# Ten of sixteen gates computed in pairs by seven block products, and a new order of the kernel's opening

## The chip, the cores and the metric

The kernel runs on one core of one Trainium2 chip. The metric is the device time of one execution in microseconds; the time before is the median of three runs, 1073.86 us (1072.72 to 1075.79). The engines are called by short names: PE (TensorE, the matrix products), PEld (its weight loads), DVE (VectorE), ACT (ScalarE), POOL (GpSimd) and SP (SyncE, whose queue issues every DMA of this kernel).

## The reference, cut to what matters

One layer of a hybrid decoder for 512 prompt tokens and 8 samples of 8 tokens, together 576 tokens, all in float32:

```python
h = rmsnorm(x, norm1_g)                       # 1024 channels
z = h @ w_in                                  # mLSTM, RWKV and gate columns
hm = mlstm(z[..., :M_END])  ;  y_a = hm @ w_branch_m
yr = rwkv7(z[..., R_START:R_END]) ; y_b = yr @ w_branch_r
gates = sigmoid(z[..., G_START:])             # 2 x 1024 columns
merged = gates[..., :1024] * y_a + gates[..., 1024:] * y_b
x = x + merged @ w_out
u = rmsnorm(x, norm2_g) @ f_up                # causal conv, gelu, gating
x = x + (gelu(conv(u[..., :D_FF])) * u[..., D_FF:]) @ f_down
x = x + sigmoid(rmsnorm(x, ple_norm_g) @ ple_gate_w) * (pe @ ple_proj)
```

followed by a last norm; the states of both branches are returned as well. The change touches the first norm, the first tiles of `h @ w_in`, and `gates`.

## The kernel before

**Layout.** Activations lie with channels on the 128 partitions and the 576 tokens along the free axis, in two halves of 288 columns (`HF`). The 1024 input channels are 8 blocks k. Each float32 operand is split into a high part and a low remainder (ACT casts the high part, DVE subtracts it), and a product takes three matrix products: high x high, high x low, low x high. `dense` computes one tile of 128 output channels: 8 blocks x 3 products x 2 halves, 48 products of 288 columns, into two PSUM banks. `wload` brings its weights in two pieces of 128x512 (256 KB each), casts (line 169) and subtracts (line 170).

**PSUM.** `bank(tag)` hands out banks by tag: three of `d`, two of `r`, and one each of `s`, `c` and `m`. In later stages the list `turn` rotates tag `d` over other tags; during the mixers it is empty.

**The opening** (lines 373 to 463). x comes in 16 loads of 144 KB (8 blocks, 2 halves). Three tiles of `w_in` lead: 12 and 13 (RWKV's low-rank columns) and 0. They are multiplied with x times the norm's gain, not yet normalised, and scaled by the norm's reciprocal root `rs` when they are evicted. Eight products on zeros (line 394) stand ahead. For each half, the squares of x are summed (ACT squares, POOL adds), `rms_half` adds them over the partitions by three one-column products, takes the root on POOL and spreads it by three transposes into a PSUM bank. Then `norm_half` writes the normalised and split x, `xs1`, and the two gate inputs of the mLSTM (`lps["if"]`, line 458) and tile 4 are computed from it.

**The mixers.** `PLAN` lists the steps in program order: `x a d b s c` with a pair's number are the RWKV steps of a pair of heads (inputs, preparation, the serial inverse of the diagonal blocks on DVE, the middle products, the samples, the output), `m` is an mLSTM head (four dense tiles and its chain), and `g` one gate tile. Sixteen gates i = 2m + b are dense tiles of `w_in`, whose result goes through tanh (line 1209) and a store (line 1210) to a buffer in device memory, `d_th[i]`, read back when the branches are merged. A gate depends on `xs1` alone, so it can stand wherever PE would otherwise wait. The order of the code sets priorities; a planner reorders the instructions of each engine when the kernel is built, by its own estimate of times. At run time each engine keeps that order.

**The buffers.** The RWKV steps use pool `rwkv` (`rp`), most tags with one buffer. `AR` and `bon` have two. `BK` is also used as `XA`, read by the middle products (line 809); `UVM` by the samples (line 886); `t1` to `t5`, `xr`, `xk`, `xv`, `xw`, `xa` by the preparation. After the plan the pool is closed and the branch stage's tiles lie in its memory.

**The FFN** already multiplies by seven block products (`seven`, from line 287). Two output tiles and two halves of the tokens form a 2x2 block matrix product with the two halves of the input channels; it takes 8 block products in the plain way and 7 by forming sums of weights (`plus`) and sums of inputs (`mixed`, line 274, once per stage). Each block product is 4 blocks x 3 products. The seven weights are split anew (lines 294 and 295), and the results are put together from banks by additions on DVE (lines 322, 327 and the caller's).

Of the kernel before, what the change touches and what calls it, by code (L numbers as in the profile page):

```python
# [15 lines left out]
P = 128  # L16
# [14 lines left out]
PLAN = "x0 a0 d0 x1 b0 a1 d1 s0 c0 g0 m0 b1 g1 x2 a2 d2 s1 c1 m1 g2 b2 x3 a3 d3 g3 s2 c2 b3 g4 g5 s3 m2 g6 c3 g7 m3 g8 g9 g10 g11 g12 g13 g14 g15".split()  # L31
# [64 lines left out]
def build(tc, nc, I, O):  # L96
# [12 lines left out]
    with st0:  # L109
# [119 lines left out]
        def rms_half(pl, acc, hf, pt="m"):  # L229

            pm = bank(pt)
# [7 lines left out]
            b = bank(pt)  # L239
# [34 lines left out]
        def mixed(tiles, pl, b11, b12, b21, b22, k, T4):  # L274

            n1, n2, t3, n4 = (pl.tile([P, HF], F32, tag=t, name="tt", bufs=2) for t in ("u2", "u2", "u3", "u3"))
# [4 lines left out]
            for name, t, e in (("n2", n2, V), ("n1", n1, G), ("t3", t3, V), ("n4", n4, V)):  # L281
                h, l = (tiles[name + a][:, k, :] for a in "hl")
# [4 lines left out]
        def seven(srca, srcb, x4, sp):  # L287
# [10 lines left out]
            def plus(a, b, e):  # L298
                t = sp.tile([P, 4, P], F32, tag="ws", name="ws", bufs=3)
                e.tensor_tensor(t, a, b, ALU.add)  # L300
                return t
# [7 lines left out]
            def tile(tag):  # L309
                return sp.tile([P, HF], F32, tag=tag, name=tag, bufs=2)  # L310

            a11, a21, a22, a12 = wdma8(srca, 0), wdma8(srcb, 0), wdma8(srcb, 4), wdma8(srca, 4)
            A, F, E, Dm = (bank("d", "pd") for _ in range(4))
            w11 = parts(a11)
            prod(A, w11, x4["b11"])
            u3 = tile("u3")
# [4 lines left out]
            u2 = tile("u2")  # L321
# [54 lines left out]
        with ExitStack() as stn:  # L376
# [14 lines left out]
            S.copy(warm[:, 0:1], nhalf)  # L391
# [17 lines left out]
            wdma(2, 0)  # L409
            wdma(2, 1)  # L410
# [3 lines left out]
            lws = [wsplit(raw[0], KD, npool, ("nh", "nl"), 6)]  # L414
            def raw_split(k, hf):
# [1104 lines left out]
```

## Time and profile before

| | |
|---|---|
| median of three runs | 1073.86 us |
| the profiled execution | 1070.66 us |
| its span, first to last instruction | 1068.8 us |
| mean granted clock of PE | 0.996 |
| PE busy | 1045.1 us, 98% |
| DVE busy | 777.0 us, 73% |
| ACT busy | 508.8 us, 48% |
| POOL busy | 254.5 us, 24% |
| DMA | 114.74 MB, mean 107 GB/s |

The profile is one execution, about 2 us longer than its span. Busy time of PE counts a product from issue to its modelled end, and products overlap, so two stretches that are both "busy" can hold different numbers of products. A group of instructions is shown by line, engine, operation and tile, with its count, its busy time, the mean of one, and what ended the idle time ahead of it. A window row gives, for one stretch, the busy time and count of each engine, the granted clock (1.00 is full), the share of the 16 DMA engines and the GB/s.

### The profile page before, as it was taken

What the parts mean: (1) busy time and instruction counts of PE and PEld (TensorE: products, weight loads), DVE (VectorE), ACT (ScalarE), POOL (GpSimd) and SP (SyncE); (2) the same over time, 40 slices, a digit from 0 to 9 for tenths busy, and PEclk for the clock granted to TensorE, in tenths of its full rate; (3) what the DMA queues carried; (4) which work ended last, traced back from release to release, by engine and by line L of the source; (5) the groups of instructions that cost most, each with busy time, mean ns of one, the idle gap of its engine ahead of it and who ended that gap; (6) DMA issues with size and microseconds to landing.
All of it is one profiled execution on the core that took longest, in us unless ns stands there. A gap on an engine that the chain in (4) does not pass through costs nothing.

```text
span 1068.8 us, 23108 instructions
## 1 busy us (share of the span) xinstructions
PE 1045.1 (98%) x8991; PEld 1009.0 (94%) x8991; DVE 777.0 (73%) x1645; ACT 508.8 (48%) x1072; POOL 254.5 (24%) x394
## 2 busy tenths in 40 slices
PE   8899999999999999999999999999999999999996
PEld 7899999999989988999999999999999999999996
DVE  7887657876786676356775799945998569975864
ACT  7684634462553344334343465522565236553822
POOL 7622112221131021001401253200343005410300
PEclk9999999999999999999999999999999999999999
DMA  7243412442342322446850312322233322342513
GB/s 252 95 127 93 108 53 58 103 141 60 88 143 75 81 84 91 143 151 234 263 181 1 116 37 93 110 90 75 85 99 97 102 70 90 94 117 67 165 40 123
DMA packets 90894, 114.74 MB, mean 107 GB/s; under 512 B 35617, under 2 KB 45217, under 8 KB 90785
## 3 DMA queue, kind: packets, MB, share of 16 engines
q1 hardware_dynamic: 90784, 113.27, 34.7%
q8 instruction: 70, 1.15, 0.4%
q14 instruction: 40, 0.32, 0.1%
HBM read 94.79 MB, written 18.45 MB: 106 GB/s over the span
## 4 chain that ended last, share of the span: by engine, by line
PE 90%; DVE 4%; DMA 4%; ACT 1%; issue 1%; SPq 0%; POOLq 0%; DVEq 0%; ACTq 0%
PE pd L193 55%; PE pd L306 20%; PE pm L655 1%; PE pm L1106 1%; PE pm L1136 1%; PE pm L835 1%; PE pm L809 1%; DMA yin<-d_y 1%; PE pm L910 1%; DVE xnf L268 1%; PE pm L917 1%; PE pm L1199 1%; PE pm L775 0%; DMA d_y<-og 0%; DMA wr<-i_w_out 0%
## 5 line engine op out<-in xcount | busy, mean ns | idle before, releaser
L169 ACT CAST wh<-wr 128x512 fp32r<-128x512 f32 (+2 forms) x170 | 101.7, 599 | 173.4 <-PE pd L193 140.7
L170 DVE TENSOR_TENSOR wl<-wr,wh 128x512 fp32r<-128x512 f32 (+2 forms) x170 | 118.8, 702 | 82.4 <-ACT wh L169 80.8
L193 PE MATMUL pd<-actl,wh 128*128 128x288 f32 x384 | 111.9, 295 | 0.0
L193 PE MATMUL pd<-acth,wl 128*128 128x288 f32 x384 | 111.4, 295 | 0.0
L193 PE MATMUL pd<-acth,wh 128*128 128x288 f32 x384 | 110.3, 295 | 0.0
L193 PEld LDWEIGHTS pd<-actl,wh 128*128 128x128 f32 x384 | 71.8, 188 | 0.0
L193 PEld LDWEIGHTS pd<-acth,wl 128*128 128x128 f32 x384 | 71.6, 188 | 0.0
L193 PEld LDWEIGHTS pd<-acth,wh 128*128 128x128 f32 x384 | 71.1, 188 | 0.1
L294 ACT CAST wh<-ws 128x512 fp32r<-128x512 f32 x76 | 47.1, 619 | 48.9 <-PE pd L306 24.8
L295 DVE TENSOR_TENSOR wl<-ws,wh 128x512 fp32r<-128x512 f32 x76 | 58.1, 765 | 8.4 <-ACT wh L294 7.9
L300 POOL TENSOR_TENSOR ws<-wr 128x512 f32<-128x512 f32 x19 | 31.7, 1670 | 96.9 <-DVE wl L295 54.1
L294 ACT CAST wh<-wr 128x512 fp32r<-128x512 f32 x57 | 35.3, 619 | 38.5 <-PE pd L306 24.0
L1333 POOL COPY o_f<-u 128x2 f32<-128x2 f32 x22 | 26.6, 1209 | 110.8 <-DVE u L1330 109.2
L295 DVE TENSOR_TENSOR wl<-wr,wh 128x512 fp32r<-128x512 f32 x57 | 39.5, 693 | 7.3 <-ACT wh L294 7.2
L216 POOL TENSOR_TENSOR rsc<-rsc,nhalf 128x3 f32<-128x3 f32 x8 | 9.3, 1167 | 131.1 <-DVE rsc L235 131.1
L1342 DVE SCALAR_TENSOR_TENSOR y<-u,vec,y 128x592 f32<-128x592 f32 x44 | 38.5, 875 | 1.2 <-ACT y L1340 1.0
L253 ACT ACTIVATE sq<-res 128x288 f32<-128x288 f32 x40 | 17.7, 445 | 36.0 <-DVE res L1279 18.5
L193 PE MATMUL pd<-mgh,ol 128*128 128x288 f32 x112 | 33.0, 296 | 0.0
L193 PE MATMUL pd<-mgl,oh 128*128 128x288 f32 x112 | 33.0, 295 | 0.0
L193 PE MATMUL pd<-mgh,oh 128*128 128x288 f32 x112 | 32.8, 295 | 0.0
L1370 DVE TENSOR_TENSOR res<-res,pd 128x288 f32<-128x288 f32 x48 | 20.9, 450 | 15.7 <-PE pd L193 15.5
L193 PE MATMUL pd<-xa0h,wh 128*128 128x288 f32 x86 | 26.4, 307 | 3.0 <-ACT zr L352 1.6
(825 smaller groups left out, 3949.4 us busy)
## 6 DMA issues: line engine op xcount, KB each, us to landing
wr<-i_w_in SPq DMA_DIRECT2D x92, 256.0 KB
wr<-i_f_up SPq DMA_DIRECT2D x88, 256.0 KB
wr<-i_f_down SPq DMA_DIRECT2D x32, 256.0 KB
d_th<-gst SPq DMA_DIRECT2D x16, 288.0 KB
th<-d_th SPq DMA_DIRECT2D x16, 288.0 KB
wr<-i_w_br SPq DMA_DIRECT2D x16, 256.0 KB
wr<-i_w_out SPq DMA_DIRECT2D x16, 256.0 KB
wr<-i_ple_gate SPq DMA_DIRECT2D x16, 256.0 KB
```

Of the source, the lines that this page charges most:

```text
L169: S.copy(wh[:, 0:nk, :], wr[:, 0:nk, :])
L170: V.tensor_tensor(wl[:, 0:nk, :], wr[:, 0:nk, :], wh[:, 0:nk, :], ALU.subtract)
L193: TE.matmul(pm[:, 0:HF], w[:, k % 4, :], a[:, c], start=k == 0 and i == 0, stop=k == n - 1 and i == 2)
L253: S.activation(sq, x[:, c], AF.Square)
L268: V.scalar_tensor_tensor(xn, xt[k][:, c], vcol(gname, k), rs, ALU.mult, ALU.mult)
L294: S.copy(wh, w)
L295: V.tensor_tensor(wl, w, wh, ALU.subtract)
L300: e.tensor_tensor(t, a, b, ALU.add)
L306: TE.matmul(pm[:, 0:HF], w[a][:, k, :], xs[k][b], start=not more and k == 0 and i == 0, stop=k == 3 and i == 2, skip_group_check=more)
L1333: G.tensor_copy(o_f[:, j, 0:2], u[:, TP:TP + 2])
L1342: V.scalar_tensor_tensor(y, u[:, i:i + 592], w(i), y, ALU.mult, ALU.add)
L1370: V.tensor_tensor(x1[m][:, c], x1[m][:, c], pss[hf][:, 0:HF], ALU.add)
```

## The change

Gates 0 to 5 stay single tiles. Gates 6 to 15 become five pairs p3 to p7; pair p computes gates 2p and 2p + 1 with `seven`. A new step t0 (`mix_x`) stands after s3 and makes the mixed inputs once: it adds high and low part of `xs1` (DVE and POOL), forms the sums and splits them, in buffers of the RWKV pool that pair 3 no longer needs. `seven` and `mixed` are given functions that hand out tiles, so that both stages can use them; in the gates' stage the fourth bank of a pair is of tag `r`. The weight sums lie in the tags `Z`, `At` and `QS`, the half results in `zr`.

In the opening, the copy on ACT writes a tile of its own, so that the zero products no longer wait for it. The six weight pieces of the three leading tiles come among the loads of x's first half, ahead of the constants and of x's second half. The splits of x's first half and of all three weights are written ahead of the squares, and the first half's products ahead of the norm. `rms_half` uses one bank for the sums and the broadcast, which stays there until `norm_half` has read it. The gate inputs get the banks `s` and `m`, and tile 8 is computed along with tile 4, in the two banks `r`.

```diff
-PLAN = "... g4 g5 s3 m2 g6 c3 g7 m3 g8 g9 g10 g11 g12 g13 g14 g15".split()
+PLAN = "... g4 g5 s3 t0 m2 c3 m3 p3 p4 p5 p6 p7".split()
...
         def rms_half(pl, acc, hf, pt="m"):
-            pm = bank(pt)
+            b = bank(pt)
+            pm = b[:, HF:HF + 3]
...
-            S.copy(warm[:, 0:1], nhalf)
+            S.copy(npool.tile([P, 1], F32, name="warm1"), nhalf)
...
-            xdma(0, 0)
-            wdma(0, 0)
-            xdma(1, 0)
-            xdma(2, 0)
-            wdma(0, 1)
-            for k in range(3, KD):
-                xdma(k, 0)
+            for what in "x0 w00 x1 x2 x3 w01 x4 x5 w10 x6 x7 w11 w20 w21".split():
+                if what[0] == "x":
+                    xdma(int(what[1]), 0)
+                else:
+                    wdma(int(what[1]), int(what[2]))
             SY.dma_start(cst, I["cst"])
-            wdma(1, 0)
-            wdma(1, 1)
             for k in range(KD):
                 xdma(k, 1)
             SY.dma_start(vec[:, KD:NV], I["vec"][:, KD:NV])
-            wdma(2, 0)
-            wdma(2, 1)
...
-            xr = []
+            xr = [raw_split(k, 0) for k in range(KD)]
+            lws.append(wsplit(raw[1], KD, npool, ("nh", "nl"), 6))
+            lws.append(wsplit(raw[2], KD, npool, ("nh", "nl"), 6))
             for k in range(KD):
-                xr.append(raw_split(k, 0))
                 add_squares(npool, acc, xt[k], k, 0, G)
-            S.copy(rsr[:, half(0)], rms_half(npool, acc, 0, "m"))
-            lws.append(wsplit(raw[1], KD, npool, ("nh", "nl"), 6))
-            for k in range(KD):
-                add_squares(npool, acc, xt[k], k, 1, G)
-            S.copy(rsr[:, half(1)], rms_half(npool, acc, 1, "m"))
-            lws.append(wsplit(raw[2], KD, npool, ("nh", "nl"), 6))
             for k in range(KD):
                 for i, j in enumerate(lead):
                     half_k(lps[j][0], lws[i], xr[k], k, KD, slice(0, HF))
+            rs0 = rms_half(npool, acc, 0, "m")
             for k in range(KD):
                 xr.append(raw_split(k, 1))
-            norm_half(npool, xt, rsr[:, half(0)], 0, "norm1_g", xs1)
+            norm_half(npool, xt, rs0, 0, "norm1_g", xs1)
+            S.copy(rsr[:, half(0)], rs0)
+            for k in range(KD):
+                add_squares(npool, acc, xt[k], k, 1, G)
             for i, j in enumerate(lead):
                 for k in range(KD):
                     half_k(lps[j][1], lws[i], xr[KD + k], k, KD, slice(0, HF))
+                if i == 1:
+                    rs1 = rms_half(npool, acc, 1, "d")
...
-            w4 = wload(I["w_in"][4], KD)
-            lps["if"] = [bank("d", "pd")]
-            lps[4] = [bank("d", "pd")]
-            lps["if"].append(bank("r", "pd"))
-            lps[4].append(bank("d", "pd"))
+            more = [4, 8]
+            wm = [wload(I["w_in"][j], KD) for j in more]
+            lps["if"] = [bank("s", "pd"), bank("m", "pd")]
+            lps[4] = [bank("d", "pd") for _ in range(2)]
+            lps[8] = [bank("r", "pd") for _ in range(2)]
...
+        def mix_x(_):
+            at = {}
+            tags = [("AR", 2, 2), ("BK", 1, 2), ("UVM", 1, 1), ("bon", 2, 1)] + [(t, 1, 1) for t in ("t1", "t2", "t3", "t4", "t5", "xr", "xk", "xv", "xw", "xa")]
+            free = []
+            for t, b, n in tags:
+                tl = rp.tile([P, n, 2, HF], F32R, tag=t, name="x4m", bufs=b)
+                free += [tl[:, i] for i in range(n)]
+            for k in (2, 0):
+                for n in ("n4", "t3", "n1", "n2"):
+                    for a in "hl":
+                        at[n + a, k] = free.pop(0)
...
+            for k in range(4):
+                xk = []
+                for e, (h, l) in zip((V, G), (xs1[k], xs1[k + 4])):
+                    t = rp.tile([P, T], F32, tag="zr", name="xsum", bufs=2)
+                    e.tensor_tensor(t, h, l, ALU.add)
+                    xk += [t[:, half(0)], t[:, half(1)]]
+                mixed(lambda n, k: at[n, k & 2][:, k & 1, :], tmp, *xk, k, x4m)
...
+        def gate_pair(p):
...
+            b1, u2, b2, b3, u3, last = seven(*(I["w_in"][RT + 16 + 8 * i + p] for i in range(2)), x4m, halves, wsum)
+            ta, tb = (mp.tile([P, T], F32, tag="gst", name="gst", bufs=2) for _ in range(2))
+            h0, h1 = half(0), half(1)
+            S.activation(ta[:, h0], b1[:, 0:HF], AF.Tanh, scale=0.5)
+            V.tensor_tensor(tb[:, h1], b2[:, 0:HF], u3, ALU.add)
+            last()
+            V.tensor_tensor(tb[:, h0], b3[:, 0:HF], u3, ALU.subtract)
+            S.activation(tb[:, h0], tb[:, h0], AF.Tanh, scale=0.5)
+            S.activation(tb[:, h1], tb[:, h1], AF.Tanh, scale=-0.5)
+            SY.dma_start(d_th[2 * p + 1], tb)
+            V.tensor_tensor(ta[:, h1], b2[:, 0:HF], u2, ALU.add)
+            S.activation(ta[:, h1], ta[:, h1], AF.Tanh, scale=0.5)
+            SY.dma_start(d_th[2 * p], ta)
```

More of the change, by code (lines that the diff above doesn't have):

```diff
@@ L271, in norm_tile, with mixed @@
             return xn
-        def mixed(tiles, pl, b11, b12, b21, b22, k, T4):
-            n1, n2, t3, n4 = (pl.tile([P, HF], F32, tag=t, name="tt", bufs=2) for t in ("u2", "u2", "u3", "u3"))
+        def mixed(at, tmp, b11, b12, b21, b22, k, T4):
+            n1, n2, t3, n4 = tmp()
             V.tensor_tensor(n1, b11, b12, ALU.subtract)
@@ L281, in mixed @@
             for name, t, e in (("n2", n2, V), ("n1", n1, G), ("t3", t3, V), ("n4", n4, V)):
-                h, l = (tiles[name + a][:, k, :] for a in "hl")
+                h, l = (at(name + a, k) for a in "hl")
                 S.copy(h, t)
@@ L285, in mixed, with seven @@
                 T4[name].append((h, l))
-        def seven(srca, srcb, x4, sp):
+        def seven(srca, srcb, x4, halves, wsum):
             def parts(w):
@@ L307, in prod @@
                                   stop=k == 3 and i == 2, skip_group_check=more)
-            def tile(tag):
-                return sp.tile([P, HF], F32, tag=tag, name=tag, bufs=2)
             a11, a21, a22, a12 = wdma8(srca, 0), wdma8(srcb, 0), wdma8(srcb, 4), wdma8(srca, 4)
-            A, F, E, Dm = (bank("d", "pd") for _ in range(4))
+            A, F, E, Dm = (bank(t, "pd") for t in ("d", "d", "d", "d" if turn else "r"))
+            u2, u3 = halves()
             w11 = parts(a11)
             prod(A, w11, x4["b11"])
-            u3 = tile("u3")
             S.copy(u3, A[:, 0:HF])
@@ L1210, in gate, with tmp @@
             SY.dma_start(d_th[i], th)
+        x4m = {n: [] for n in ("n1", "n2", "t3", "n4")}
+        def mix_x(_):
[9 more added lines that the diff above has]
+                        at[n + a, k] = free.pop(0)
+            def tmp():
+                a, b = (mp.tile([P, 2, HF], F32, tag="gst", name="tt", bufs=2) for _ in range(2))
+                return a[:, 0], a[:, 1], b[:, 0], b[:, 1]
+            for k in range(4):
[5 more added lines that the diff above has]
+                mixed(lambda n, k: at[n, k & 2][:, k & 1, :], tmp, *xk, k, x4m)
+            for n, k0, hf in (("b11", 0, 0), ("b21", 4, 0), ("b22", 4, 1)):
+                x4m[n] = [tuple(t[:, half(hf)] for t in xs1[k]) for k in range(k0, k0 + 4)]
@@ new lines, in build, with halves, wsum @@
+        sums = ["Z", "At", "QS"]
+        def gate_pair(p):
+            def halves():
+                t = rp.tile([P, 2, HF], F32, tag="zr", name="hh", bufs=2)
+                return t[:, 0], t[:, 1]
+            def wsum():
+                sums.append(sums.pop(0))
+                return rp.tile([P, 4, P], F32, tag=sums[-1], name="ws")
+            b1, u2, b2, b3, u3, last = seven(*(I["w_in"][RT + 16 + 8 * i + p] for i in range(2)), x4m, halves, wsum)
[11 more added lines that the diff above has]
+            SY.dma_start(d_th[2 * p], ta)
@@ L1306, in build, with half_tiles, wsum @@
         x4 = {n: [] for n in ("n1", "n2", "t3", "n4")}
+        def half_tiles(*tags):
+            return lambda: [fp.tile([P, HF], F32, tag=t, name="tt", bufs=2) for t in tags]
+        def wsum():
+            return fp.tile([P, 4, P], F32, tag="ws", name="ws", bufs=3)
         xt4 = {n + a: fp.tile([P, 4, HF], F32R, tag="x4", name=n + a, bufs=8) for n in x4 for a in "hl"}
@@ L1324, in up @@
             else:
-                b1, u2, b2, b3, u3, last = seven(I["f_up"][j], I["f_up"][NFF + j], x4, fp)
+                b1, u2, b2, b3, u3, last = seven(I["f_up"][j], I["f_up"][NFF + j], x4, half_tiles("u2", "u3"), wsum)
                 V.tensor_tensor(ac[:, HF:T], b2[:, 0:HF], u3, ALU.add)
```

23 lines of the change are left out of this document (12 added, 11 removed).

## The prediction

> **What bounds the kernel now.** I read the page's span and chain of waits first, then stretches of the span side by side, then the opening instruction by instruction, and last the groups of VectorE instructions of the FFN, which already computes by the seven products that the gates are to get.
>
> ```profile
> span 1068.8 us, 23108 instructions
> ...
> PE 90%; DVE 4%; DMA 4%; ACT 1%; issue 1%; SPq 0%; POOLq 0%; DVEq 0%; ACTq 0%
> ```
>
> TensorE (PE) holds 90% of the chain that ends last. So a product that is not issued counts in full, as long as the others can feed PE at the shorter time. A stretch's busy column can't say whether they do, because it also counts slow products; the number of products in a stretch can.
>
> ```profile
> 0.00:16.00 16.00, 12.01 (x41) 9.77 (x42) 10.17 (x14) 12.68 (x29) 11.16 (x26) 0.89 0.84 266
> ...
> 420.00:488.00 68.00, 68.00 (x567) 65.20 (x566) 32.76 (x73) 23.38 (x50) 6.65 (x12) 1.00 0.44 145
> ...
> 700.00:740.00 40.00, 40.00 (x304) 40.00 (x303) 17.26 (x31) 9.12 (x15) 1.28 (x1) 1.00 0.28 86
> ```
> ```profile
> 343.00:488.00 145.00, 143.50 (x1453) 132.80 (x1452) 85.84 (x205) 54.26 (x125) 18.41 (x36) 1.00 0.37 112
> ```
>
> The columns are the stretch, then busy time and count of PE, PEld, DVE, ACT and POOL, granted clock, DMA share and GB/s. From 700 to 740 nothing disturbs PE: 304 products in 40.00 us, **0.1316 us each**, the price of a 288-column product from here on. The stretch from 343 to 488 is that of gates 6 to 15 with the end of RWKV pair 3 and of mLSTM heads 2 and 3: PE is full (143.50 of 145), VectorE has 59 us of air. The opening is where PE is poor: 41 products up to 16 us, those on zeros included.
>
> **Gates as pairs: products.** Gates 6 to 15 are ten dense tiles of 8 blocks x 3 products x 2 halves = 48, together 480. A pair is 7 block products of 4 x 3, or 84, and five pairs are 420. That removes 60 products x 0.1316 = **-7.9 us** of PE. The weights loaded stay 20 pieces of 256 KB and the stores to the gates' buffers stay ten, so no DMA is added and the SP queue gets no longer there.
>
> **Gates as pairs: who feeds them.**
>
> ```profile
> L295 DVE TENSOR_TENSOR wl<-ws,wh 128x512 fp32r<-128x512 f32 x76 | 58.1, 765 | 8.4 <-ACT wh L294 7.9
> L300 DVE TENSOR_TENSOR ws<-ws,wr 128x512 f32<-128x512 f32 x38 | 25.8, 680 | 0.3
> L1326 DVE TENSOR_TENSOR ac<-pd,u 128x288 f32<-128x288 f32 x19 | 8.5, 447 | 0.1
> L284 DVE TENSOR_TENSOR n2l<-tt,n2h 128x288 fp32r<-128x288 f32 x4 | 3.0, 754 | 0.0
> ```
> ```profile
> 634.34 0.44 DVE L284 TENSOR_TENSOR n2l<-tt,n2h 128x288 fp32r<-128x288 f32 x1
> 634.71 0.82 DVE L1342 SCALAR_TENSOR_TENSOR y<-u,vec,y 128x592 f32<-128x592 f32 x1
> ...
> 638.26 0.67 DVE L300 TENSOR_TENSOR ws<-ws,wr 128x512 f32<-128x512 f32 x1
> 638.86 0.67 DVE L295 TENSOR_TENSOR wl<-wr,wh 128x512 fp32r<-128x512 f32 x1
> ```
> ```profile
> L170 DVE TENSOR_TENSOR wl<-wr,wh 128x512 fp32r<-128x512 f32 (+2 forms) x170 | 118.8, 702 | 82.4 <-ACT wh L169 80.8
> ```
>
> A pair costs VectorE seven weight splits, three weight sums (the fourth is POOL's) and five evictions of 288 columns. By mean durations that is 7 x 0.765 + 3 x 0.680 + 5 x 0.447 = 9.6 us. Queued instructions overlap, though: the timeline starts a 512-wide one 0.60 us after the last (638.26 to 638.86) and a 288-wide one after 0.37 (634.34 to 634.71), which makes 10 x 0.60 + 5 x 0.37 = 7.9 us. PE needs 84 x 0.1316 = 11.1 us for a pair, so in a steady run VectorE keeps up. The new step t0 adds four sums of 576 columns (0.765 x 576 / 512 = 0.86 each, an estimate) and 24 instructions of 288: between 3.4 + 24 x 0.37 = 12.3 and 3.4 + 24 x 0.754 = 21.5 us. The single gates' 20 splits go, 14.0 us at 0.702 or 12.0 at 0.60. VectorE in this stretch then has 85.8 - 12.0 + 39.3 + 12.3 = 125 us to do at the low end and 85.8 - 14.0 + 48.2 + 21.5 = 142 at the high one, in 145 - 7.9 = 137 us. I take the low end, since a full queue is what it will have; but 91% leaves little air for the chains of pair 3 and head 3, whose instructions stand in the same queue. ScalarE gets 15 casts more and t0's 16 on 54 us of 145, POOL five sums and t0's twelve on 18: both stay off the path.
>
> What thin air costs, the start of the FFN shows, where the same mixing step and the first seven-product tiles fall together:
>
> ```profile
> 620.00:640.00 20.00, 18.45 (x137) 17.98 (x137) 20.00 (x41) 13.18 (x27) 8.70 (x11) 1.00 0.12 40
> 640.00:660.00 20.00, 19.61 (x148) 19.38 (x148) 19.71 (x37) 10.67 (x20) 4.78 (x6) 1.00 0.32 106
> ```
>
> 285 products in 40 us against 304: 19 x 0.1316 = 2.5 us lost, VectorE full. I take **+2.5 us** as what is given back. The ends are 0 (all of t0 hides under heads 2 and 3) and the whole hole of the third rival, below.
>
> **The opening.**
>
> ```profile
> 0.93 0.27 DVE L390 MEMSET warm<- 128x256 f32 x1 [0.93 <-PEq L1513]
> ...
> 2.82 3.78 PE L394 MATMUL pm<-warm 128*128 128x256 f32 x8 [2.82 <-ACT warm L391]
> ...
> 3.63 0.54 ACT L417 ACTIVATE xrh<-x,vec 128x288 fp32r<-128x288 f32 x1 [0.85 <-DMA x<-i_x]
> ...
> 4.70 0.62 ACT L154 CAST nh<-wr 128x512 fp32r<-128x512 f32 x1 [0.54 <-DMA wr<-i_w_in]
> ...
> 6.04 0.80 PE L193 MATMUL pd<-xrh,nh 128*128 128x288 f32 x1
> ```
> ```profile
> 13.00:14.00 1.00, 1.00 (x5) 0.76 (x5) 1.00 (x2) 1.00 (x4) 0.99 (x2) 0.50 1.10 354
> ```
>
> The eight zero products wait for ScalarE's copy (line 391) and run from 2.82 to 6.60, over the moment at which the first real product could go (its weight is cast at 4.70 + 0.62 = 5.32). They now wait for the zeroing alone (done at 1.20), start at about 1.3 and are gone by 5.1. Up to 16 us PE does 41 - 8 = 33 real products, 4.3 us at the pace, out of 9.96 since 6.04: **5.6 us lost**, some of it at the half clock (0.50 from 13 us on) behind sparse products. What is missing is work: tile 12 alone is fed, because the constants, and for the third tile x's second half too, are queued ahead of the other weights. The new order puts all six weight pieces and x's first half in front: 6 x 256 + 8 x 144 = 2688 KB, at 266 KB a us landed near 1.3 + 10.1 = 11.4. ScalarE then needs 8 x 0.54 + 6 x 0.62 = 8.0 us from 3.63, so the last piece is ready near 12.5, with the squares moved behind. By then tile 12's 24 products and half of tile 13's are done; the other 36 take 4.7 us, so the first half's 72 are through by about 17.5. At the old rate it would be 33 + 1.5/0.1316 = 44. The difference, 28 x 0.1316 = 3.7 us, I round to **-4 us** with what the earlier zero products bring. The ends are 0 and -5.6. Behind it x's second half is later by 512 KB, 1.9 us at that rate, and POOL's squares of the first half start later; both are needed only once those 72 products are done.
>
> By the Trainium skill (TensorE: Matmul & The Clock Gate, What's actually happening), the clock is granted after a busy window of about 3.4 us and withdrawn after an idle one; the 0.50 agrees. By that rule zero products that end earlier could leave the thin start at half clock for longer, some ten products at twice the price, an estimate of 1.3 us, and the sum would be -2.7 here; I leave it at -4.
>
> Two stalls stand later in the opening:
>
> ```profile
> 40.78 0.37 PE L193 MATMUL pd<-xa0h,wh 128*128 128x288 f32 x1 [1.42 <-DVE k L978]
> ...
> 50.84 0.40 PE L193 MATMUL pd<-xa0h,wh 128*128 128x288 f32 x1 [1.56 <-ACT zr L352]
> ```
>
> The first waits for a bank that the gate inputs hold; they move to banks s and m. But the second halves of tiles 4 and 8 now need the banks of tiles 12 and 0, which come free only when VectorE has evicted them with the second norm. One wait of this size replaces the other; I count 0 (ends -1.4 and +3.0, both stalls over again). Tile 8's 48 products only move forward. The norm's sum and its broadcast in one bank of PSUM follow each other anyway: 0.
>
> **Sum.** -7.9 + 2.5 - 4 = -9.4 us. The profiled execution took 1070.66 us, 1.9 over its span, so 1061.3 by it. It lies 3.2 under the median of the runs shown, 1073.86; against that the sum gives **1064.5 us**.
>
> **Rivals.**
>
> 1. *All of it arrives*: t0 hides, the early loss and the first bank stall vanish. -7.9 - 5.6 - 1.4 = -14.9: **1059**. For it: 59 us of air on VectorE. Against: the FFN paid 2.5 for the same step.
>
> 2. *The new order of the opening isn't what runs.* A planner orders the instructions when the kernel is built: the product at 40.78 waits for line 978, which the code reaches only after the opening. If it orders squares and splits as before, the opening gains nothing, -7.9 + 2.5 = -5.4: **1068.5**. Against: the loads, which set the early loss, stand in one queue and had nothing to wait for.
>
> 3. *The hole doesn't close (slower).*
>
> ```profile
> 349.10 0.41 ACT L1209 ACTIVATE gst<-pd 128x288 f32<-128x288 f32 x1 [4.85 <-PE pd L193]
> ...
> 425.21 0.41 ACT L1209 ACTIVATE gst<-pd 128x288 f32<-128x288 f32 x1 [2.60 <-PE pd L193]
> ```
> ```profile
> 404.84 1.08 PE L886 MATMUL pm<-UVM,B 128*64 128x512 f32 x4
> 409.82 1.09 PE L809 MATMUL pm<-XA,Q 64*64 64x128 f32 x16
> ```
>
> Gate 6's first half is evicted at 349, gate 8's at 425. The 96 products of gates 6 and 7, 12.6 us, fill PE while pair 3 is in VectorE's serial part. A pair needs mixed inputs that lie in pair 3's buffers UVM and XA, read until 405 and 410. If the chain comes no sooner, pairs start where gate 8's products do, 24 x 0.1316 ahead of its eviction or some more, about 420. Then PE has 5 x 11.1 in place of 8 x 6.3 us (+4.7), and VectorE from 420 on 32.8 - 16 x 0.702 + 48.2 + half of t0 (8.4, between its ends) = 78.2 us in 68 + 4.7 (+5.5). With the opening's -4 that is +6.2: **1080**. It decides once the first pair's products with mixed inputs begin after about 416. Against: with the filler gone the chain waits less behind dense products, and heads 2 and 3 (eight dense tiles) can fill. By the Trainium skill (SBUF — State Buffer, SBUF: two separate sides), VectorE with two SBUF inputs and POOL exclude each other from a shared port for whole instructions. The mixing rows agree (0.754 mean where 0.44 stands for the same shape), so t0's POOL part speaks for this rival.
>
> 4. *It closes by half*: the gates come to nothing, -4: **1070**.
>
> **Numbers.** Chances: forecast 0.38, rivals 0.15, 0.20, 0.12 and 0.15 in their order. 0.3% is 3.2 us, what a measurement of this kernel can tell; faster means under 1070.6. Faster: 0.37 + 0.15 + 0.15 + 0.08 = 0.75; the same: 0.01 + 0.05 + 0.06 + 0.01 = 0.13; slower 0.12, the third rival and the tail of the fourth. The range runs from 1057 (the first rival less 2) to 1075 (the fourth plus a second bank stall of 3 and 2 of its own).
>
> **What would show it.** 60 products fewer from 343 on, and the pace of 0.1316 us between p3 and p7; t0's VectorE group near 3 to 5 us per block. If PE shows waits for weight splits or mixed inputs of over 5 us in all, the give-back was too small. Up to 16 us some 60 real products instead of 33 and a clock of 1.00 from 12 to 16; fewer than 45 prove the second rival. The first eviction of a pair after 420 would prove the third.

## The result: 2.5% slower, and the profile after

The changed kernel takes 1101.30 us (median of four, 1096.91 to 1104.55) where the kernel before takes 1074.44 (median of four, 1072.72 to 1075.79). The ratio is 1.0249, 95% interval 1.0219 to 1.0280: 26.9 us slower. Forecast were 1064.5 and a range of 1057 to 1075, with a chance of 0.12 for slower. Three executions at a mean granted clock of 0.85, 0.74 and 0.55 (1129.85 us of the kernel before, 1285.44 of e3, 1683.81 of e8) are left out of every median, difference and ratio below.

The page of the changed kernel: its span, the slices of PE's granted clock (40 slices of 27.5 us each), the chain of waits.

```profile
span 1100.0 us, 23179 instructions
...
PEclk8999999999989977998999999999999999999999
...
PE 45%; DVE 3%; issue 0%; ACT 0%; DVEq 0%; ACTq 0%
```

Before, all forty slices had a clock of 9. Now the first slice is at 8, and there are dips at 303 to 330 us, 385 to 440 and 495 to 523. (This chain was followed back over less than half of the span, so its shares aren't set beside those of before.) The stretches that the prediction showed of before, now of after, the FFN's shifted by the 32 us that it begins later (columns as there: stretch, busy time and count of PE, PEld, DVE, ACT, POOL, granted clock, DMA share, GB/s):

```profile
0.00:16.00 16.00, 12.22 (x39) 9.54 (x40) 10.06 (x14) 11.37 (x25) 9.54 (x25) 0.74 0.80 262
...
343.00:488.00 145.00, 135.50 (x1367) 121.97 (x1366) 114.12 (x254) 60.39 (x141) 34.92 (x49) 0.89 0.28 81
...
652.00:672.00 20.00, 18.47 (x138) 17.99 (x136) 20.00 (x42) 12.96 (x27) 9.11 (x12) 1.00 0.13 41
672.00:692.00 20.00, 19.60 (x146) 19.37 (x147) 19.71 (x36) 10.78 (x20) 4.77 (x6) 1.00 0.33 107
732.00:772.00 40.00, 40.00 (x304) 40.00 (x304) 16.89 (x32) 9.21 (x15) 1.68 (x1) 1.00 0.28 86
```

The FFN is untouched: 304 products in 40 us and 138 + 146 = 284 at its start, as before (304 and 285). Between 343 and 488 it isn't: 1367 products instead of 1453, PE idle for 9.5 us instead of 1.5, the clock at 0.89. VectorE has gone from 86 to 114 us, and yet PE isn't fed. (Forecast were 125 to 142, but for all of the pairs; now the last pair's products start as late as 505.9.)

Where the time goes shows in the start of the same PE work in the traces (us; "opening" and "pairs" are the two halves of the change run alone, below):

| first product of | before | after | late | opening alone, late | pairs alone, late |
|---|---|---|---|---|---|
| pair 0's inputs AR, BK | 94.0 | 101.8 | 7.8 | 5.9 | 0.3 |
| pair 2's | 249.7 | 259.8 | 10.1 | 5.9 | 0.4 |
| pair 3's | 334.2 | 350.3 | 16.1 | 6.3 | 9.8 |
| pair 3's TT, X | 377.3 | 398.0 | 20.7 | 3.6 | 16.5 |
| the branches (y0h) | 485.3 | 515.0 | 29.7 | 2.7 | 23.0 |
| the FFN (xb0h) | 613.5 | 645.9 | 32.4 | 2.5 | 24.8 |

(Each column is one profiled execution. That of the opening alone is the quickest of its kernel, so its column is a low estimate.) Three places, then: the opening, the stretch from pair 2's end to the last gate, and the passage to the branches. The same stretches, before first, then after:

```profile
380.00:400.00 20.00, 19.30 (x267) 17.15 (x267) 15.23 (x40) 7.88 (x21) 6.93 (x11) 1.00 0.19 60
400.00:420.00 20.00, 19.20 (x223) 16.66 (x216) 14.14 (x29) 9.47 (x21) 3.29 (x8) 1.00 0.30 97
420.00:440.00 20.00, 20.00 (x197) 19.13 (x196) 6.86 (x16) 5.28 (x11) 0.18 (x1) 1.00 0.49 160
440.00:460.00 20.00, 20.00 (x148) 18.43 (x148) 7.74 (x18) 5.75 (x13) 1.14 (x4) 1.00 0.29 88
```
```profile
380.00:400.00 20.00, 16.97 (x205) 14.98 (x206) 17.10 (x47) 5.03 (x16) 8.76 (x9) 0.92 0.25 51
400.00:420.00 20.00, 18.48 (x242) 14.97 (x239) 13.95 (x29) 8.95 (x20) 2.24 (x2) 0.57 0.13 43
420.00:440.00 20.00, 15.05 (x184) 12.99 (x183) 15.80 (x29) 7.30 (x18) 9.02 (x11) 0.77 0.14 48
440.00:460.00 20.00, 20.00 (x138) 18.68 (x138) 15.66 (x31) 10.09 (x22) 2.42 (x5) 0.97 0.55 172
500.00:520.00 20.00, 15.36 (x95) 14.45 (x94) 12.16 (x22) 10.38 (x21) 2.33 (x4) 0.83 0.73 246
```

Before, VectorE's air lies from 420 to 460 (6.9 and 7.7 us busy of 20): there gates 8 and up run, and need little of it. From 380 to 420 VectorE has 5 to 6 us of air in 20, and over half of PE's busy time goes to dense products. They show in PE's groups of line 193 from 375 to 435, one of the 24 groups of before and of after:

```profile
L193 PE MATMUL pd<-xa0h,wh 128*128 128x288 f32 x10 | 3.0, 296 | 0.0
```
```profile
L193 PE MATMUL pd<-xa0h,wh 128*128 128x288 f32 x3 | 1.0, 331 | 0.0
```

All 24 together were 239 products and are 87. (Moved along with pair 3's TT, X, by 20.7 us to 395.7 to 455.7, the stretch has 24 of them after, and 101 products of pairs.) So most of the cover of pair 3, the work that PE could do beside it, is gone; the average over 145 us hid that it was there. Now the first mixed product runs at 440.52 and the first pair is evicted at 446.98; in PE's timeline:

```profile
440.52 1.01 PE L306 MATMUL pd<-x4m,wh 128*128 128x288 f32 x4
```

### The profile page after: what moved, and what is told of

The parts are those of the page before. It is cut to its first block, busy times and chain, and to the rows that moved or that the text cites. A ratio compares the mean times of both kernels' runs of the same rounds, so it can differ in the third digit from the quotient of the medians.

```text
span 1100.0 us, 23179 instructions
## 1 busy us (share of the span) xinstructions
PE 1060.5 (96%) x8931; PEld 1020.1 (93%) x8931; DVE 828.1 (75%) x1728; ACT 525.3 (48%) x1108; POOL 280.9 (26%) x411
## 5 line engine op out<-in xcount | busy, mean ns | idle before, releaser
L169 ACT CAST wh<-wr 128x512 fp32r<-128x512 f32 (+2 forms) x150 | 89.0, 596 | 152.6 <-PE pd L193 124.3
L170 DVE TENSOR_TENSOR wl<-wr,wh 128x512 fp32r<-128x512 f32 (+2 forms) x150 | 105.6, 709 | 55.7 <-ACT wh L169 54.0
L294 ACT CAST wh<-ws 128x512 fp32r<-128x512 f32 x96 | 59.4, 620 | 72.8 <-PE pd L306 37.0
L295 DVE TENSOR_TENSOR wl<-ws,wh 128x512 fp32r<-128x512 f32 x96 | 72.3, 754 | 10.4 <-ACT wh L294 9.8
L300 POOL TENSOR_TENSOR ws<-wr 128x512 f32<-128x512 f32 x24 | 39.4, 1642 | 143.4 <-DVE wl L295 90.9
L294 ACT CAST wh<-wr 128x512 fp32r<-128x512 f32 x72 | 44.6, 619 | 47.6 <-PE pd L306 32.0
L295 DVE TENSOR_TENSOR wl<-wr,wh 128x512 fp32r<-128x512 f32 x72 | 51.1, 709 | 11.4 <-ACT wh L294 10.0
L216 POOL TENSOR_TENSOR rsc<-rsc,nhalf 128x3 f32<-128x3 f32 x8 | 7.1, 886 | 130.9 <-DVE rsc L236 130.9
L306 PE MATMUL pd<-x4m,wh 128*128 128x288 f32 x160 | 34.5, 307 | 0.0
L300 DVE TENSOR_TENSOR ws<-ws,wr 128x512 f32<-128x512 f32 x48 | 33.0, 687 | 0.4
```

Source lines behind the costliest of these rows:

```text
L169: S.copy(wh[:, 0:nk, :], wr[:, 0:nk, :])
L170: V.tensor_tensor(wl[:, 0:nk, :], wr[:, 0:nk, :], wh[:, 0:nk, :], ALU.subtract)
L216: G.tensor_tensor(t, t, nhalf[0:t.shape[0], :].to_broadcast([t.shape[0], n]), ALU.pow)
L294: S.copy(wh, w)
L295: V.tensor_tensor(wl, w, wh, ALU.subtract)
L306: TE.matmul(pm[:, 0:HF], w[a][:, k, :], xs[k][b], start=not more and k == 0 and i == 0, stop=k == 3 and i == 2, skip_group_check=more)
```

## The experiments

Theory A: the price is t0. Once gates 6 to 15 need mixed inputs, hardly a dense product is left that covers pair 3's serial part on VectorE, and t0 adds its own VectorE work there. Rivals: B, an accident of the plan or of a buffer, mended by two single gates ahead, a third buffer, or another place of the steps; C, the opening; D, the passage to the branches. Differences in us are between medians of one comparison.

### The two halves alone

```diff
 e1_opening: the diff without PLAN, mix_x, gate_pair, seven and mixed
 e2_pairs:   the diff without the opening's parts
```

> Only the opening is new, the gates and the order of the mixers stay as before. Theory A (the loss is the sum of two separate ones): the profile after is already 7.8 us late at the first AR,BK products of pair 0 (101.8 for 94.0) and 10.5 at pair 1, where no gate pair has run, so this kernel is 8 to 10 us slower than before, about 1083. Theory B (the opening delays a stretch that later waits swallow; the loss of the whole is the pairs' alone): within 3 us of before, 1071 to 1077.

> The old opening, with the step t0 and the five pairs. Theory A: the gates' stretch and the passage to the branches lose 17 to 22 us by themselves, so 1092 to 1096. Theory B: all of the loss is here, 1099 to 1103. The prediction's own sum for this part was -5.4, about 1069.

The opening alone: 1078.94, +5.2 us, ratio 1.0048 (1.0024 to 1.0072). Its executions scatter (1073.28 to 1083.79), and the profiled one is the quickest of them. The pairs alone: 1095.77, +22.0, ratio 1.0236 (1.0179 to 1.0292). 5.2 + 22.0 = 27.2 for the measured 26.9: within these intervals the halves add up, and C is a fifth of the loss.

### The opening

What the opening pays is the place of one line, next to the bank stalls that the prediction counted as 0. In the timeline of the kernel before, and then of the opening alone, the tile that scales the leading tiles' results is copied and then used by their evictions on VectorE:

```profile
27.51 0.39 ACT L425 COPY rsz<-pm 128x288 f32<-128x288 f32 x1
...
30.65 0.45 DVE L355 TENSOR_TENSOR rsz<-pd,rsz 128x288 f32<-128x288 f32 x1
```
```profile
33.88 0.39 ACT L428 COPY rsz<-pm 128x288 f32<-128x288 f32 x1
35.56 0.45 DVE L355 TENSOR_TENSOR rsz<-pd,rsz 128x288 f32<-128x288 f32 x1
...
36.06 0.61 PE L193 MATMUL pd<-xa0h,wh 128*128 128x288 f32 x1 [0.35 <-DVE rsz L355]
```

The new order writes this copy behind `norm_half`; it runs 6.4 us later, the evictions 4.9, the leading tiles keep their banks longer, and tile 4 starts only behind them. PE's own waits in the gap ahead of 36.06 are 1.4 us for the norm's transposes, 1.1 us for a normalised x and 0.4 us for the eviction, so the bank need not be the whole of it: the order that the planner made of it can have a part too. So the copy was moved ahead of the norm again, and in a second kernel the squares were made to wait for the last split:

```diff
 e7_copy (opening alone, and)
+            S.copy(rsr[:, half(0)], rs0)
             norm_half(npool, xt, rs0, 0, "norm1_g", xs1)
-            S.copy(rsr[:, half(0)], rs0)
 e8_copy_sq (e7, and the squares of the first half scaled by a 1
 that VectorE derives from the last split)
```

> The new opening alone (1078.9), with one line moved: the copy of the first half's reciprocal root into rsr stands ahead of the first norm, not behind it. Theory: the evictions of the leading tiles' first halves need this copy, which ran at 33.88 (27.51 before); the next tiles' products need those banks, so PE stood from 32.2 to 36.1 and then ran at the half clock until 39. With the copy early the evictions run by 31, the gap falls to under 1.5 us and the first products of the recurrence come 3 to 5 us earlier: 1074 to 1076. Rival: the gap belongs to the second half's norm (its transposes stand in PE's queue ahead of the next products), and the evictions only follow: 1077 to 1080.

> As the kernel before it, and the squares of x's first half take their scale from a column that VectorE writes after the last split of that half, so that they stand behind the splits in fact as the source has them. Theory (shared port): VectorE's splits of x followed each other by 0.97 us instead of 0.44 to 0.50 wherever POOL added squares at the same time, and set the pace of 3 products per 0.97 us up to 16 us, in both kernels; with POOL quiet they take 0.45 to 0.6 us, over 50 real products are through by 16 us instead of 33, and the leading tiles end 2.5 to 4 us earlier (28 to 29.5): 2 to 4 us below the kernel with only the copy moved. Rival (the prediction's: x and the weights arrive too late): the splits wait for their loads instead, the count to 16 us stays under 45 and the time within 1 us.

With the copy back in its place: 1072.75, ratio 0.9984 (0.9967 to 1.0001), 6.2 us better than the opening alone. The stretch after the leading tiles, first of the opening alone, then with the copy moved:

```profile
32.00:36.00 4.00, 1.20 (x6) 0.51 (x5) 4.00 (x10) 3.44 (x9) 2.42 (x4) 0.95 0.00 0
```
```profile
32.00:36.00 4.00, 4.00 (x32) 4.00 (x32) 3.62 (x9) 1.94 (x5) 2.46 (x3) 1.00 0.26 87
```

6 products become 32, and pair 0 starts at 94.3 instead of 99.8. So one line cost what the opening lost; but of the forecast -4 no more than 1.2 us came either (1072.75 for 1073.94, not clear of the noise). The second kernel shows why. VectorE's splits and POOL's adds in the kernel before, then with the squares held back:

```profile
8.85 4.42 DVE L418 SCALAR_TENSOR_TENSOR xrl<-x,vec,xrh 128x288 fp32r<-128x288 f32 x5
9.13 3.83 POOL L254 TENSOR_TENSOR acc<-acc,sq 128x288 f32<-128x288 f32 x4 [1.02 <-ACT sq L253]
```
```profile
9.65 0.94 DVE L413 SCALAR_TENSOR_TENSOR xrl<-x,vec,xrh 128x288 fp32r<-128x288 f32 x2
...
16.23 9.73 POOL L254 TENSOR_TENSOR acc<-acc,sq 128x288 f32<-128x288 f32 x10
```

Alone a split takes 0.47 us, beside POOL's adds 0.97 from one to the next (the products that follow it start at 9.42, 10.40 and 11.38). By the Trainium skill (SBUF — State Buffer, SBUF: two separate sides), a VectorE instruction with two SBUF inputs and a GpSimd one that reads SBUF lock each other out of a shared port for a whole instruction; the rows agree: five splits and four adds run side by side in these 4 us, and each split costs twice its time. Held back, the squares leave the first half to run as forecast, 64 products up to 16 us (8 on zeros) and a clock of 1.00:

```profile
0.00:16.00 16.00, 13.67 (x64) 11.51 (x65) 7.83 (x17) 10.49 (x21) 4.07 (x19) 1.00 0.83 264
```

But POOL's ten adds now run from 16 to 26, the norm comes later, PE is idle for 3.4 of the 16 us from 20 to 36 (82 products, 124 with the copy alone moved), and the kernel takes 1080.68 (1.0072, 1.0049 to 1.0096), 7.9 us more than without this edit. The early loss was real, its recovery is paid back behind the norm.

```diff
 e16_no8 (e7, and tile 8 back in the mixers)
-            more = [4, 8]
+            more = [4]
```

> The new opening with its copy moved (1072.8), and tile 8 back among the mixers, so that its 48 products stand again where they stood before. Theory (filler): with tile 8 moved forward PE had nothing between 74 and 79 us, waited 1 us for a square and ran at 0.57 from 78 to 82 (99 products from 70 to 86 in place of 128 before shows what was lost there); with tile 8 back this stall goes: 2 to 3 us below, 1069.5 to 1071.5, faster than before by 0.2 to 0.4%. Rival (the stall is the sparse chain's own): within 1 us of 1072.8.

1072.06, ratio 0.9993 (0.9980 to 1.0006): tile 8's place makes no difference.

### The end of the gates and the passage to the branches

In every kernel with five pairs PE starves between 500 and 520 (93 to 109 products). The queue of SP in the changed kernel, at the first of the last pair's two stores:

```profile
507.50 0.33 SPq L1256 DMA_DIRECT2D d_th<-gst  x1
507.92 0.38 SPq L1281 DMA_DIRECT2D yin<-d_y  x1
```

The branches' first loads, `yin`, are issued right behind it. In the pairs alone the last mixed product starts at 498.85 and the first branch product at 508.26; before, the last gate product was at 485.13 and the first branch product at 485.27.

```diff
 e4_tail (pairs alone, and)
-s3 t0 m2 c3 m3 p3 p4 p5 p6 p7
+s3 t0 m2 c3 m3 p3 p4 p5 p6 g14 g15
 e6_yin (pairs alone, and yin in memory of its own)
```

> As the kernel with the old opening and the pairs, but the last pair is two single gates, 14 and 15, which need none of the RWKV pool's buffers. If the passage to the branches is late because the branches' y tiles lie in memory that the last pairs still use and their loads stand behind the last weights and stores, the loads are issued while the two dense tiles run, and the 9 us lost between the last mixed products and the first branch products come back: 1083 to 1087. If that passage is not the cause, 1 to 2 us slower than with five pairs (12 products more): 1093 to 1098.

> As the kernel with the old opening and five pairs (1095.8), but the four y tiles that the branches load first lie in memory that no pair uses (that of G0, G4 and G1). Theory: their loads are issued once pair 3's outputs are stored, 20 us or more ahead of the last pair's end, the wait at 500 to 520 goes, and the first branch product follows the last mixed product by 1 to 3 us instead of 9.4: 1086 to 1090, with all five pairs kept. Rival: the loads stand behind the last weights in SP's queue whatever their memory, or the y splits' own buffers (those of the weight sums) hold them: 1093 to 1096.

With two plain gates at the end: 1087.44 (1.0142, 1.0100 to 1.0184), 8.3 us better than the pairs alone although it has 12 products more. The stretch, pairs alone and then with the tail:

```profile
500.00:520.00 20.00, 14.79 (x93) 13.87 (x93) 12.73 (x24) 8.07 (x14) 2.34 (x4) 0.83 0.88 299
```
```profile
500.00:520.00 20.00, 20.00 (x153) 20.00 (x153) 14.46 (x29) 7.30 (x13) 2.38 (x4) 1.00 0.87 297
```

So D is part of it. Memory isn't the reason for the late loads: with `yin` in tiles that were free, the time is 1096.08 (1.0206, 1.0181 to 1.0231) and the loads still stand behind that store, at 502.20. What puts them there stays open.

### Other places for t0: two or four single gates ahead, a third buffer

```diff
 pairs alone, and PLAN from s3 on:
 e3_fill        s3 t0 m2 g6 c3 g7 m3 p4 p5 p6 p7
 e9_fill2       s3 m2 g6 c3 g7 t0 m3 p4 p5 p6 p7
 e10_fill4      s3 m2 g6 c3 g7 m3 g8 g9 t0 p5 p6 p7
 e11_fill4_tail s3 m2 g6 c3 g7 m3 g8 g9 t0 p5 p6 g14 g15
 e12_all        the same plan as e11, with e7's opening
 e5_gst3        the plan of after, three buffers gst instead of two
```

> As the kernel with the old opening and the pairs, but gates 6 and 7 stay single tiles at their old places, and only gates 8 to 15 are pairs (48 products fewer than before instead of 60). If the missing filler makes the hole (third rival), products of gates 6 and 7 run while pair 3 is in VectorE's serial part, the clock stays at 1.00 from 380 to 440, and the first branch product comes 10 us or more earlier than with five pairs: 1078 to 1084. If VectorE's load by splits and sums of the pairs is the limit, the loss shrinks only by a fifth: 1088 to 1092.

> As the kernel with the old opening and five pairs (1095.8), but the buffers that gates, the mixing step's temporaries and the pairs' results share (tag gst) are three instead of two. Theory: the mixing step's fourth sum waited 5.3 us on VectorE for the store of gate 5, with the chains of pairs 2 and 3 queued behind it, and made pair 3's first products 9.8 us late (343.97 for 334.2). With a third buffer it waits for gate 4's store, long done: no such wait, pair 3's first products within 3 us of before, and 1086 to 1090. Rival: pair 3 is late because the mixing step's own work stands ahead of it on VectorE; then the wait goes, but less than 3 us come back: 1093 to 1096.

> Old opening; gates 6 and 7 single as in the earlier run that kept them (1107), but the mixing step stands behind them in the plan. Theory: there the two gates' results had to wait for the two gst buffers, which the mixing step ahead of them held until 421; their banks stayed full, and PE stood. Now the two gates are evicted near 349 to 363 as before, PE has no stall of 7 us at 385 to 392 and the time is 15 us or more lower: 1082 to 1092. Rival (VectorE is too full with four pairs and the mixing, whatever the order): 1100 or more.

> Old opening; gates 6 to 9 single at their old places, then the mixing step and three pairs (36 products fewer than before). Theory (filler): in the kernel before 192 products of gates 6 to 9 were through by 436 and filled PE while pair 3 was in its serial part; with five pairs only some 60 dense products ran from 375 to 435, the clock fell to 0.5 and the work moved behind. With the four gates back, the clock from 375 to 435 is 1.00 and pair 3's last state product is within 3 us of before (454.3). What stays is the passage to the branches (9 us) less 4.7 for the products: 1075 to 1081. Rival (the mixing step and the pairs on VectorE cost what they cost, wherever they stand): 1085 or more.

> As the run with gates 6 to 9 single, but gates 14 and 15 are single as well and stand last, so only two pairs are left (24 products fewer, 3.2 us). Theory: with filler ahead and plain gates behind, both losses are gone and the products saved show: 1070 to 1073, at or below before. Rival (a pair does not pay even where nothing else is in the way, because VectorE's splits and sums hold PE up): 1076 or more.

> The same plan of gates (6 to 9 single, two pairs, 14 and 15 single) with the new opening and its copy moved ahead of the norm (that opening alone: 1.2 us below before). If both parts are independent, 1 to 2 us below the same plan with the old opening: 1069 to 1072, faster than before by 0.2 to 0.4%. If the planner's order of the mixers shifts with the opening, as it did between openings already (pair 1 to pair 3 moved by up to 6 us), anything within 4 us of that.

Single gates behind t0 in the code (e3) make it worse: 1106.14, 1.0303 (1.0275 to 1.0331), above both forecasts. By the code t0 holds the two buffers that the gates' results need; in the trace gates 6 and 7 are evicted only from 421.75 on, when t0's last splits run, where it was 349 before. PE has 91 products in 20 us, with one wait of 7.3 us on ACT (line 1152), whose queue has waited 8.8 us for VectorE's serial work while no gate fills:

```profile
380.00:400.00 20.00, 8.17 (x91) 5.76 (x88) 13.74 (x41) 4.41 (x12) 6.88 (x7) 0.66 0.30 64
```

A third buffer (e5) shortens t0's own wait for a store on VectorE (5.3 us in the pairs alone, until 299.14) to 3.0 us, until 301.63. Pair 3 comes no sooner (351.2, where the pairs alone had 344.0), and the time is 1092.01, 1.0172 (1.0128 to 1.0216): 3.8 us less, with intervals that overlap, and between the two forecasts.

With the two gates ahead of t0 (e9): 1086.37, 1.0100 (1.0068 to 1.0133), the best place found with the old opening. With four ahead (e10, e11, e12): 1109.81, 1103.20 and 1082.84, ratios 1.0325, 1.0266 and 1.0075. None of the gains expected of them came. In all three t0 then stands where little cover is left; the row of e12, the best of them:

```profile
440.00:460.00 20.00, 16.90 (x70) 12.45 (x69) 19.54 (x40) 8.20 (x21) 13.53 (x14) 0.63 0.14 47
```

VectorE is full with t0 and PE gets under half of its products, at a clock of 0.63. e11 and e12 have the same plan for the gates and differ by 20 us; e7's opening by itself is worth 1 of them, and 5 are there when pair 3 starts (345.8 in e11, 340.9 in e12). The rest isn't taken apart here; the planner's order of each kernel is the likely cause, not a shown one.

### t0 by itself, and the tail

```diff
 e13_t0_alone   s3 m2 g6 c3 g7 t0 m3 g8 g9 g10 g11 g12 g13 g14 g15
 e14_fill2_tail s3 m2 g6 c3 g7 t0 m3 p4 p5 p6 g14 g15
 e15_all        e14's plan, e7's opening, three buffers gst
```

e13 multiplies all gates as before and leaves t0's results unused.

> Old opening, all sixteen gates single, and the mixing step t0 alone, behind gate 7 and before head 3, its results used by nothing. Theory 1 (the mixing step is what costs; the pairs themselves only lack filler): with every gate there as filler it still makes pair 3 late, and the time is 6 to 12 us above before, 1080 to 1086. Theory 2 (the mixing step hides where there is filler; what costs is that gates 8 to 15 no longer come early): within 3 us of before, 1072 to 1077, and the kernel with the same order and four pairs (1086.4) owes its 12 us to the pairs.

> Old opening; gates 6 and 7 single, then the mixing step, pairs 4 to 6, and gates 14 and 15 single at the end. If the gain of the plain tail (8.3 us with four pairs ahead of it) adds to that of the order with gates 6 and 7 ahead of the mixing (1086.4): 1077 to 1080. If the passage to the branches was late only because the pairs were, 1084 or more.

> The same plan with the new opening, its copy moved ahead of the norm, and three gst buffers. If the steps are independent: 1.2 us less for the opening and 3.8 less for the third buffer, 1072 to 1076, about equal to before. If they aren't (the planner orders each kernel anew), up to 8 us above that.

t0 alone: 1087.20, +14.8 us, ratio 1.0128 (1.0108 to 1.0147). With four pairs at the same place (e9) it was +11.9: 2.9 us better by the medians (the two intervals overlap), where four pairs remove 48 x 0.1316 = 6.3 us of products. So at this place t0 is the whole loss, and pairs earn back a part of what they save at most. Its rows:

```profile
300.00:320.00 20.00, 20.00 (x165) 15.86 (x167) 10.03 (x21) 5.34 (x12) 3.67 (x8) 0.57 0.14 47
380.00:400.00 20.00, 15.16 (x126) 13.32 (x125) 18.60 (x32) 6.19 (x16) 8.76 (x8) 0.83 0.34 80
```

Against 251 and 267 products before. From 380 to 400 that is t0. The first row lies ahead of t0's splits (the first starts at 377.7) and comes back below. Most of this loss arises there, for pair 3 is already 13.1 us late when it starts (347.2), and the branches are 19.1 us late in the same trace. So e13 does not show that the gates' independence is what counts: all sixteen gates are independent in it, 195 of the 239 dense products still run from 375 to 435, and 14.8 us are lost all the same.

e14, the tail with the best place, takes 1083.84, 1.0097 (1.0080 to 1.0115), no better than e9's ratio, and e15 1087.77, 1.0148 (1.0119 to 1.0177): gains of single edits didn't add up once the plan had moved.

### The sums out of pair 2's chain

Up to VectorE's 414th instruction the pairs alone and the kernel before run the same order. Then t0's first sums stand in pair 2's serial chain (they take buffers `zr` that come free there). The first store of pair 2's inverse is issued at 289.5 instead of 284.3, and PE waits longer for what is read back, which was 1.5 us before. Its wait there in the pairs alone, and then with the edit below:

```profile
PE pm L771 <- DMA TT<-scr0t: 2.9, 1, 2.9
```
```profile
PE pm L771 <- DMA TT<-scr0t: 0.5, 1, 0.5
```

The sums were given other buffers, free only later:

```diff
 e17_sums_late (pairs alone, and)
-for e, (h, l) in zip((V, G), (xs1[k], xs1[k + 4])):
-    t = rp.tile([P, T], F32, tag="zr", name="xsum", bufs=2)
+for e, tag, (h, l) in zip((V, G), ("G0", "G1"), (xs1[k], xs1[k + 4])):
+    t = rp.tile([P, T], F32, tag=tag, name="xsum")
 e18_best (e14 with the same edit)
```

> The kernel with the old opening and five pairs (1095.8), but the sums of the mixing step lie in the buffers of G0 and G1 instead of zr, so that the first of them can't stand before pair 3 has used those. Theory (trigger): the orders of the engines are those of before up to the first sum, which stands on VectorE at 246.9 and on POOL at 281.4, inside pair 2's serial chain; from there the order is another, the chain's transposes through memory are issued 4.8 us later, PE waits 2.8 us for them instead of 1.5, and the clock is at 0.50 to 0.66 until 308 to 315. Without the early sums the stretch up to 320 is that of before, pair 3's first products come within 2 us of 334.2 and 7 to 10 us are saved: 1086 to 1089. Rival: the whole order is shuffled by any step t0, and the loss reappears elsewhere: 1093 to 1099.

> The plan with gates 6 and 7 ahead of the mixing step, pairs 4 to 6 and gates 14 and 15 single at the end (1083.8), with the sums in G0 and G1. If order, tail and trigger are separate losses, 7 to 9 us below that: 1075 to 1077, still not faster than before, since the mixing step takes VectorE from pair 3's chain or from the pairs wherever it stands. If the mixing step can be hidden after all, 1070 or less.

```profile
300.00:320.00 20.00, 20.00 (x247) 18.62 (x246) 16.28 (x34) 11.33 (x24) 9.72 (x14) 0.91 0.36 119
...
420.00:440.00 20.00, 17.05 (x99) 13.09 (x94) 19.28 (x36) 8.93 (x21) 13.84 (x13) 0.66 0.34 107
```

That place heals: 247 products from 300 to 320 (202 in the pairs alone), pair 3 starts at 336.6 instead of 344.0, and the last of its products of Sa and MT, which carry its state, start at 446.1 instead of 461.1 (454.3 before). The time doesn't move: 1097.39, 1.0243 (1.0209 to 1.0276), as this run's rival said. t0's casts and splits now run from 419 to 448, with VectorE full and PE at 99 products in 20 us. e18 takes 1088.44, 1.0143 (1.0095 to 1.0192), no gain either. So pair 3's chain is in time without its cover; what is lost is PE's time beside it and beside t0. Two places so different with one price speak for A against B, but don't settle it: with early sums the loss stands mostly ahead of t0's splits, with late sums at t0 itself, where gates 8 and up, being pairs, can't run beside it. A kernel with t0 alone, its sums late and all sixteen gates single, would tell the two apart and was not run. What is shown is that no place tried hides t0.

## Why the prediction was wrong

**The step that failed is the give-back of +2.5 us**, and with it "VectorE has 59 us of air". The air was there, but as an average over stretches of two kinds. From 380 to 420 VectorE is busy for 14 to 15 us in 20 with pair 3, and single gates keep PE busy without it; from 420 to 460 VectorE has 12 to 13 us of air in 20, under plain gates. The change takes the gates of the first kind away, and t0 must be done before any gate of the second kind can run. The start of the FFN was the wrong measure: there VectorE's splits of mixed inputs start from 612.9 to 637.5, beside dense tiles that need none of them (line 193), and the first mixed product comes at 634.2. Here VectorE's twelve splits stand in one queue with pair 3's chain. In the pairs alone the last mixed product is at 498.85 where the last gate product was at 485.13, 13.7 us later instead of 7.9 sooner: 21.6 us are given back, not 2.5. Another 9.3 us (from 498.85 to 508.26, less the 0.14 of before) lie in the passage to the branches, for which the prediction had no term; two plain gates at the end bring 8.3 of it back. -7.9 + 21.6 + 9.3 = 23.0, the lateness of the branches in the table. Of the 21.6, t0 by itself is shown (14.8 us in e13); how they divide between t0's own work, its early sums and the lost cover stays open.

**The size of t0 was right.** VectorE's splits of mixed inputs, after:

```profile
L284 DVE TENSOR_TENSOR x4m<-tt,x4m x12: 436/456/1044, 321.9 to 429.6; 128x288 fp32r<-128x288 f32 x12
```

(Shortest, median and longest in ns.) With its four sums and twelve other instructions t0 takes VectorE 17.9 us (the 28 durations added up), inside the forecast 12.3 to 21.5. That it would lie beside other work was wrong, not the price: the last split starts at 429.6, and no pair can finish before.

**The 60 products and the pace were right.** From 460 to 480 the pairs alone do 172 products, from 480 to 500 146, near the 152 of 20 us at 0.1316, with VectorE 18 us busy. In a steady run pairs feed PE, as forecast. Five of them don't pay for t0.

**Rival 3 named the mechanism and its sign of proof** (a first eviction after 420; it came at 447.0): pairs start only when pair 3 has let go of its buffers and t0 is done, and PE lacks work until then. Its price failed: +6.2 assumed that PE and VectorE are late only by their own work from 420 on, with pair 3's chain where it was. The chain came 14 us later itself (the last of its products of Sa and MT at 468.6, 454.3 before; 461.1 in the pairs alone). The argument against it, that heads 2 and 3 can fill, fell with the 87 dense products counted above.

**The opening's -4 failed at "what is missing is work, loads queued behind".** Rival 2 held: 39 products up to 16 us, eight on zeros, under the 45 that were to prove it; with the order forced (e8) they are 64. The splits, at 0.97 each beside POOL, set the early pace, not the loads. And in place of the 0 for the bank stalls, one line ahead of an eviction cost 6.2 (e1 against e7), above the upper end of +3.0: the prediction looked at which bank is asked for, not at what the eviction that frees it waits for.

## What to carry to other kernels

Read the air of an engine in stretches as short as the work that is to hide there, not over the stage: 59 us of air in 145 did not hide 18. Before a filler that depends on nothing is made cheaper by making it depend on a new step, ask where that step will stand, its first instructions included, and what PE will do beside it. Test the new step by itself first: e13 alone would have shown 14.8 us against the 7.9 to be gained. A copy that frees a bank belongs ahead of the long step that only shares its input.

## What the runs showed of the hardware that was not expected

In two traces the clock fell about 2 us after the end of a gap in PE's work, and the fall outlasted the gap several times. Stretches of e9, then of e7, then of the kernel before:

```profile
294.00:296.00 2.00, 0.00 (x0) 0.00 (x0) 0.00 (x0) 0.00 (x0) 0.00 (x0) 1.00 0.84 190
...
300.00:306.00 6.00, 6.00 (x43) 4.50 (x41) 1.91 (x6) 1.21 (x2) 0.28 (x1) 0.50 0.01 3
```
```profile
75.00:76.00 1.00, 0.22 (x2) 0.11 (x1) 1.00 (x4) 1.00 (x3) 1.00 (x1) 1.00 0.80 289
...
79.00:80.00 1.00, 1.00 (x7) 0.98 (x6) 0.85 (x2) 0.26 (x2) 1.00 (x1) 0.50 0.00 0
```
```profile
292.00:294.00 2.00, 0.97 (x9) 0.79 (x9) 0.89 (x2) 0.00 (x0) 0.00 (x0) 1.00 0.68 151
```

In e9 PE stands still for the whole of 294 to 296, and the clock is at 0.50 from 300 on, 43 products in 6 us, and at full only from 316 on; in e7 a gap of about 1.0 us around 76 is followed by 0.50 from 79 to 81; in the kernel before a longer one, the 1.5 us wait told above (1.03 us of it within 292 to 294), is followed by none up to 306. By the Trainium skill (TensorE: Matmul & The Clock Gate, What's actually happening), the clock is full or half and is set by a free-running window of about 3.4 us. Half and full agree; that a whole idle window is needed doesn't, since about 1 us sufficed once. The gap of e9 is the wait for pair 2's load told above (2.8 us there): a wait of a few us was followed by some seventeen at half clock. How much of the time lost the low clock causes, and how much of it only goes with waiting, no run here separates. An estimate for e13's row from 300 to 320: PE has no idle time there and VectorE is busy for half of it, so at a clock of 0.57 up to 20 x 0.43 = 8.6 us of the 13.1 that pair 3 is late can be the clock's.
